# A neighbourhood-attention layer: one more unit by seven products, shorter filler in each attention cycle, and other orders of the first loads and of the output rows' splits

## The chip, the cores and the metric

The kernel runs on one core of a Trainium2 chip. The metric is the device time of one execution in microseconds, the median of several runs. In the profile PE is TensorE's matmuls, PEld its weight loads, DVE is VectorE, ACT is ScalarE, POOL is GpSimd and SP issues nearly all transfers.

## What is computed

One encoder layer on 2048 tokens (a grid of 32 rows by 64 columns) with 1024 features and 16 heads of 64. All in float32:

```python
h = rmsnorm(x, norm_0)
q, k, v, gate = split(h @ w_in_0, 4)                # 1024 x 4096
# each token attends to 8 rows x 16 columns of the grid around it
s = (q . k) / 8 + bias[head, row offset, column offset]
p = softmax(s)                                      # over the 128 keys
o = p . v
x = x + (o * silu(gate)) @ w_out_0                  # 1024 x 1024
out = rmsnorm(x, norm_f)
```

## The kernel before

Each large matrix product is done in three matmuls per tile: an operand is split into a high part (ScalarE copies it, rounded) and a low part (VectorE subtracts the high part), and high x high, low x high and high x low are summed in one PSUM bank. So each operand tile costs one operation of ScalarE and one of VectorE on 512 columns. In the code these are h and l, woh and wol (output weights), gh and gl (gated attention rows), qh and ql (queries).

There are four stages.

1. `stage_one` loads x transposed in blocks (`land`, `spot`), computes the values for the first half of the tokens and then keys, queries and gates for it. Its first rows wait for data from HBM: `load_v0` and `load_x` issue the first weights and blocks on SP in a written order, `split_v` makes high and low parts of the value weights, `values_of` runs the matmuls of one block of 128 features.
2. `stage_two` does the same for the second half of the tokens. Both compute a unit (a kind k, q or g and 256 output features for 1024 tokens) with `seven_products`: seven products of quarter blocks, 84 matmuls, where the plain way takes 96. Stage two does so for the units in `units_two`; those left over (`halves`) become filler for stage three.
3. The attention stage is a loop of 33 cycles, numbered here as m in the code. Cycle m transposes the probabilities of the strip before (`turns(m-1)`, 44 small matmuls into six banks `ph`, copied to `pta` by three operations each of ScalarE and VectorE), computes the scores of the next (`scores(2m)` and `scores(2m+1)`, eight banks `s`), and then multiplies the strip before by its values (`values`, bank `o`). A strip is a pair of heads and a group of eight grid rows. Cycles 0 to 7 take the first row group of all eight head pairs, 8 to 23 the two middle ones, 24 to 31 the last. Even cycles from 8 to 22 also build tables of bias and mask (`em`) on GpSimd.
   VectorE adds the bias to the scores and takes the maximum, ScalarE takes the exponential and its sum, VectorE the reciprocal (L1040), and `normalise` scales the eight tiles of a cycle by it on GpSimd (L1044), four after the first pair of scores and four after the second.
   Between `values` of one cycle and `turns` of the next TensorE runs filler, so that it need not wait for that chain: matmuls of `projections()` (the halves) and, once these are used up, of `outputs()`. `feed(n)` runs n of them; the table `amount` says how many in each cycle, `dense` in the first 25. A group of filler is 24 matmuls into one bank (`pp` or `po`); at its end `give` or `add_rows` empties the bank. `consume(1)` splits one prefetched tile of weights.
4. `outputs()` multiplies the rows by the output weights: 32 turns of 24 matmuls. Before a row tile's first turn `split_og` makes gh and gl of it, two operations of 512 columns on each engine. `add_rows` adds x (`y`, VectorE) and squares (`xr`, ScalarE). `run_roots` computes an inverse root in eight tiny operations of VectorE, and two more scale the rows.

The order on each engine is the order in which the code is written: nothing is rescheduled. `clock` counts filler matmuls; `store(key, lag, f)` puts off a step until the clock has gone on by `lag`. A tile of weights may be split when the clock has gone on by 32 since its load was issued.

Of the kernel before, what the change touches and what calls it, by code (L numbers as in the profile page):

```python
# [70 lines left out]
def build(ctx, tc, x, xr, xt, wg, rpb, last, w_out, n0, nf, masks, out):  # L71
# [58 lines left out]
    onesr = one.tile([128, 128], F32R, name="onesr")  # L130
    rt = one.tile([128, 16], F32, name="rt")
    g0 = one.tile([128, NK], F32, name="g0")
    accs = [one.tile([128, 512], F32, name=f"acc{i}") for i in range(2)]
# [24 lines left out]
    def load_item(it):  # L158
        kind, a, b = it
        t = raws[it] = raw([128, 512], F32, "raw")  # L160
        asked_at[it] = clock[0]
# [44 lines left out]
    def stats(c):  # L206
        ss = rows.pop(c)
        m = tiny.tile([128, 8], F32, name="m")[:, :4]
        nc.vector.tensor_tensor(m, ss[:, 0:8:2], ss[:, 1:8:2], OP.add)
        nc.vector.tensor_scalar(m, m, 1.0 / D, EPS, op0=OP.mult, op1=OP.add)  # L210
        rsqrt(rt[:, 4 * c:4 * c + 4], m, 4)

    dgs = {}
# [48 lines left out]
    AHEAD = 5  # L262
    clock = [0.0]
    freed = set()
    state = dict(used=0, loaded=0, half=-1, done_halves=0, event=0.0)
# [264 lines left out]

    def split_v(u, a, b, ks=(0, 1)):
        t = VR[u, a, b].rearrange("p (k c) -> p k c", c=256)
        if a == 0 and ks[0] == 0:
# [3 lines left out]
        nc.scalar.activation(h, t[:, k], AF.Copy)  # L537
# [28 lines left out]
    def stage_one():  # L566
# [219 lines left out]
    def stage_two():  # L786
# [9 lines left out]
        def also(n, i):  # L796
            if n == 0:
                if i == 0:
                    load_ahead()
                    load_e(0, xp)[0]()  # L800
                elif i == 1:
                    load_e(0, xp)[1]()
                    load_masks()
# [166 lines left out]

    def load_e(p, pool_=None):
# [65 lines left out]

    def normalise(i):
        st = ST.pop(i)
        nc.vector.reciprocal(st[:, 8:12], st[:, 4:8])  # L1040
        for j, C in enumerate(pairs[i][2]):
            for s in range(2):
                o = 8 + 2 * j + s
                nc.gpsimd.tensor_scalar(X[i, C][s], X[i, C][s], st[:, o:o + 1], 0.5, op0=OP.mult, op1=OP.mult)  # L1044

# [234 lines left out]
    ready = dict(loaded=2, split=1, res=RES_EARLY)  # L1280

    def outputs():
        loaded_at = {1: -1e9}

# [4 lines left out]
        def ahead(k, i=0):  # L1289
            n = ready["loaded"]  # L1290
            if n < tiles and place[n] <= k + 4 and og_ready(n):
                load_og(n)
                loaded_at[n] = clock[0]
# [84 lines left out]
    def begin(m):  # L1378
# [11 lines left out]
        if m == 0:  # L1390
            bias(0, 0, 2)
            later_loads(load_e(order[1][0]), 5, 3)

# [17 lines left out]
    for m in range(cycles + 1):  # L1411
        a = amount[m]
        begin(m)
        feed(a * 0.35)
        if m:
            normalise(2 * m - 1)
        middle(m)
        if m:
            quiet[0] = True
            for k in range(3):  # L1420
                consume(1 + (m == 1), turn=True)
                feed(a * 0.11)
                if k == 1:
# [3 lines left out]
            if quiet[0]:  # L1427
                consume(1, turn=True)
                feed(a * 0.12)
                quiet[0] = False  # L1430
            else:
                feed(a * 0.12)
        else:
            feed(a * 0.45)
        feed(a * 0.2, 8)
        if m:
# [11 lines left out]
        if m:  # L1448
            values(2 * m - 2)
            values(2 * m - 1)  # L1450
        n = next_sums(m)
        if 0 < m and n and order[m][1] < 2:
            for f in load_e(order[n][0]):
                f()
# [52 lines left out]
```

## Time and profile before

| | |
|---|---|
| median of 3 runs | 1062.33 us (1062.28 to 1062.53) |
| profiled execution | 1062.42 us, span 1060.6 us |
| PE busy | 1048.6 us (99%) |
| VectorE busy | 725.7 us (68%) |
| ScalarE busy | 518.5 us (49%) |
| GpSimd busy | 312.9 us (30%) |
| granted TensorE clock | 0.999 |

The profile is that of one execution; its rows give the start from the span's begin and the duration, both in microseconds, then engine, line and operation, `out<-in` by the program's names, and in brackets how long the engine idled before and what released it. Matmul records overlap, so a matmul's cost is read from the distance of starts. In the attention stage the letter F below stands for the start of a cycle's first filler matmul.

### The profile page before, as it was taken

How to read it: one execution, taken by the hardware profiler on the slowest of the kernel's cores; microseconds unless marked ns; L12 is line 12 of the kernel's file. 1: busy time of each engine (PE TensorE's matmuls, PEld its weight loads, DVE VectorE, ACT ScalarE, POOL GpSimd, SP SyncE). 2: the span in 40 equal slices, each digit the busy share in tenths (PEclk: the TensorE clock that was granted, in tenths of full speed). 3: DMA queues.
4: the chain of work that ended last, by engine and by line, in shares of the span. 5: the costliest groups of instructions: out<-in, count | busy, mean ns of one | idle time of the engine just before them, and what ended most of it. 6: DMA issues, size and time to landing. Idle time of an engine off the chain costs nothing.

```text
span 1060.6 us, 20997 instructions
## 1 busy us (share of the span) xinstructions
PE 1048.6 (99%) x7608; PEld 877.1 (83%) x7608; DVE 725.7 (68%) x1593; ACT 518.5 (49%) x1218; POOL 312.9 (30%) x392
## 2 busy tenths in 40 slices
PE   8999999999999999999999999999999999999997
PEld 6888888887888888888888888888887888888886
DVE  5476888768897625666576667766778777686654
ACT  7645344333343334333265656666767656445422
POOL 0000221322311000000157775665756642213200
PEclk9999999999999999999999999999999999999999
DMA  8733655353635433533798778886987788777352
GB/s 309 227 100 108 190 202 179 126 149 119 184 120 154 120 100 89 170 99 129 234 300 262 239 238 246 269 268 207 297 280 251 222 282 273 255 243 247 105 155 80
DMA packets 129184, 207.58 MB, mean 196 GB/s; under 512 B 11768, under 2 KB 55544, under 8 KB 129080
## 3 DMA queue, kind: packets, MB, share of 16 engines
q1 hardware_dynamic: 128648, 205.84, 62.5%
q8 instruction: 60, 0.98, 0.4%
q10 hardware_dynamic: 432, 0.40, 0.1%
q14 instruction: 44, 0.36, 0.1%
HBM read 147.47 MB, written 58.72 MB: 194 GB/s over the span
## 4 chain that ended last, share of the span: by engine, by line
PE 91%; DVE 4%; issue 1%; POOL 1%; DMA 1%; ACT 0%; SPq 0%; POOLq 0%; DVEq 0%
PE pp L434 30%; PE pv L555 16%; PE s L1021 7%; PE o L1123 7%; PE po L1324 5%; PE po L1326 5%; PE po L1322 5%; PE pp L382 4%; PE pp L378 4%; PE pp L380 4%; PE ph L1101 4%; DVE f L417 1%; POOL x L1044 1%; DMA land<-in_xt_dram 1%; POOL em L987 1%
## 5 line engine op out<-in xcount | busy, mean ns | idle before, releaser
L1044 POOL TENSOR_SCALAR x<-x,st 128x360 f32<-128x360 f32 (+5 forms) x256 | 176.1, 706 | 222.9 <-DVE st L1040 205.0
L434 PE MATMUL pp<-h,f 128*128 128x512 f32 x576 | 186.6, 390 | 0.0
L1035 ACT ACTIVATE x<-x,st 128x360 f32<-128x360 f32 (+5 forms) x256 | 151.3, 593 | 23.7 <-DVE st L1029 23.7
L454 POOL TENSOR_TENSOR tmp<-tmp,rb 128x512 f32<-128x512 f32 x36 | 58.6, 1628 | 270.1 <-DVE tmp L452 209.4
L987 POOL TENSOR_TENSOR em<-e,mk 128x264 f32<-128x264 f32 (+3 forms) x94 | 78.0, 864 | 192.1 <-DMA mk<-in_masks_dram 189.4
L434 PEld LDWEIGHTS pp<-h,f 128*128 128x128 f32 x576 | 108.2, 188 | 22.2
L1029 DVE CUSTOM_DVE_ANT_0 x<-s,em 128x360 f32<-128x360 f32 (+5 forms) x256 | 123.8, 538 | 0.6 <-POOL em L987 0.6
L434 PE MATMUL pp<-t,f 128*128 128x512 f32 x480 | 121.7, 390 | 0.3
L434 PE MATMUL pp<-l,f 128*128 128x512 f32 x288 | 112.2, 389 | 0.0
L434 PEld LDWEIGHTS pp<-t,f 128*128 128x128 f32 x480 | 90.0, 188 | 19.6 <-DVE u L447 1.1
L1324 PE MATMUL po<-woh,gl 128*128 128x512 f32 x252 | 99.2, 394 | 1.5 <-DVE gl L1188 1.5
L1326 PE MATMUL po<-wol,gh 128*128 128x512 f32 x252 | 98.9, 393 | 0.0
L1322 PE MATMUL po<-woh,gh 128*128 128x512 f32 x252 | 98.9, 393 | 0.0
L1077 DVE COPY pta<-ph 120x512 f32<-120x512 f32 (+5 forms) x96 | 57.8, 641 | 55.4 <-PE ph L1101 55.4
L555 PE MATMUL pv<-wh,h 128*128 128x512 f32 x256 | 88.4, 391 | 1.9 <-ACT h L519 1.4
L555 PE MATMUL pv<-wh,l 128*128 128x512 f32 x256 | 88.2, 390 | 0.0
L555 PE MATMUL pv<-wl,h 128*128 128x512 f32 x256 | 88.2, 390 | 0.0
L1077 ACT ACTIVATE pta<-ph 120x512 f32<-120x512 f32 (+5 forms) x96 | 49.7, 558 | 77.0 <-PE ph L1101 76.8
L1123 PEld LDWEIGHTS o<-pta,vt 120*64 120x64 f32 (+2 forms) x1792 | 80.9, 138 | 7.4 <-DVE st L1029 5.4
L1123 PE MATMUL o<-pta,vt 120*64 120x128 f32 (+5 forms) x1792 | 85.3, 253 | 0.0
L417 DVE TENSOR_TENSOR f<-raw,f 128x512 fp32r<-128x512 f32 x90 | 69.7, 775 | 22.4 <-ACT f L416 22.4
L1021 PE MATMUL s<-kt,qh 64*128 64x480 f32 (+5 forms) x512 | 83.0, 372 | 0.5 <-DVE pta L1077 0.5
(157 smaller groups left out, 1959.5 us busy)
## 6 DMA issues: line engine op xcount, KB each, us to landing
raw<-in_wg_dram SPq DMA_DIRECT2D x126, 256.0 KB, 5.0
row<-in_xr_dram SPq DMA_DIRECT2D x32, 256.0 KB, 4.0
vd<-v SPq DMA_DIRECT2D x32, 256.0 KB, 2.4
k_hi<-hi SPq DMA_DIRECT2D x32, 256.0 KB, 2.5
k_lo<-lo SPq DMA_DIRECT2D x32, 256.0 KB, 2.9
sgd<-sg SPq DMA_DIRECT2D x32, 256.0 KB, 4.1
qr<-qd SPq DMA_DIRECT2D x32, 256.0 KB, 5.0
sgt<-sgd SPq DMA_DIRECT2D x32, 256.0 KB, 5.1
```

The costliest lines, as they stand in the source:

```text
L434: nc.tensor.matmul(B[n, P], t[:, int(m == 2), c], x[k][int(m == 1)], start=P in (1, 6, 5) and k == 0 and m == 0, stop=k == 3 and m == 2, s ...
L555: nc.tensor.matmul(ps[t], a[:, o], b, start=k == 0 and m == 0, stop=k == NK - 1 and m == 2)
L987: (nc.gpsimd if attending[0] or not s else nc.vector).tensor_tensor(sh(t), E[p, s][:, u0 + 4:u1 + 4, v0 + 8:v1 + 8].rearrange("p u (s v) - ...
L1021: nc.tensor.matmul(pst[s], qq[a, qs], kk[a, :r1 - r0, c0:c1].rearrange("p r (s c) -> p s r c", c=8), start=(m == 0), stop=(m == 2))
L1029: nc.vector.tensor_tensor_reduce(X[i, C][s], pst[s], EM[p, ROW_TYPE[T], COL_TYPE[C], s], -1.0, 1e38, OP.add, OP.min, st[:, o:o + 1])
L1035: nc.scalar.activation(X[i, C][s], X[i, C][s], AF.Exp, bias=st[:, o:o + 1], scale=-1.0, accum_out=st[:, 4 + o:5 + o])
L1044: nc.gpsimd.tensor_scalar(X[i, C][s], X[i, C][s], st[:, o:o + 1], 0.5, op0=OP.mult, op1=OP.mult)
L1077: (nc.vector.tensor_copy if h else lambda o, i_: nc.scalar.activation(o, i_, AF.Copy))(t[:k, h, b * 512:b * 512 + w], banks_[b, h][:k, :w])
L1123: nc.tensor.matmul(to.rearrange("d (h q) -> d h q", q=64) if nq > 64 else to, vt[:k, strip, s * 64:s * 64 + 64], t[:k, h, at:at + 64] if n ...
L1322: nc.tensor.matmul(p, gh, woh[q, j], start=(i == 0), stop=False)
L1324: nc.tensor.matmul(p, gl, woh[q, j], start=False, stop=False)
L1326: nc.tensor.matmul(p, gh, wol[q, j], start=False, stop=(i == NK - 1))
```

## The change

The parts of it:

- `units_two` has a seventh unit, ("k", 2), which leaves `halves`: 96 filler matmuls become 84 in stage two.
- `dense` is 24.2 where it was 28, with 1.5 more in even and 1.5 less in odd cycles from 8 to 23. In each cycle `feed` runs 10 before the second `normalise` and shares the rest out anew.
- The factor one half of the gate moves from `normalise` into the values (`rth`). The second `normalise` of a cycle does two of its four tiles on ScalarE.
- Ages of loads count 26 per cycle beside the filler (`now`), against 36 instead of 32.
- Rows of the output are split by `split_rows` in the place of a `consume`, no longer by `ahead` during the attention.
- At the start VectorE makes the first high part of one value weight, and the second block of value weights comes in halves, with one block of x ahead of the second halves.
- `load_e` loads 11 of 15 rows of the bias for the first row group.

```diff
-    units_two = [(k, j) for j in range(2) for k in "kqg"]
-    halves = [(k, j, 1, c) for j in range(2, 4) for g in (("k", "q", "g") if j == 2 else ("k", "qg")) for c in (2, 3) for k in g]
+    units_two = [(k, j) for j in range(2) for k in "kqg"] + [("k", 2)]
+    halves = [(k, j, 1, c) for j in range(2, 4) for g in (("q", "g") if j == 2 else ("k", "qg")) for c in (2, 3) for k in g]
...
+    def now():
+        return clock[0] + 26 * runs[0]
...
-            if attending[0] and clock[0] - asked_at[items[state["used"]]] < 32 and not asked:
+            if attending[0] and now() - asked_at[items[state["used"]]] < 36 and not asked:
...
-        nc.scalar.activation(v, p, AF.Copy, scale=rt[:, t:t + 1] if t < 8 else 1.0)
+        nc.scalar.activation(v, p, AF.Copy, scale=rth[:, t:t + 1] if t < 8 else 0.5)
...
         for b in (1, 2, 3):
-            for a in range(2):
-                load_v0(0, a, b, ev([128, 512], F32, "raw") if b == 3 else None)
-            for k in (2 * b, 2 * b + 1):
-                load("x%d1" % (k // 4 + 1), k % 4)
+            for j in range(2):
+                for a in range(2):
+                    if b == 1:
+                        load_v0(0, a, b, cols=parts_[j])
+                    elif j == 0:
+                        load_v0(0, a, b, ev([128, 512], F32, "raw") if b == 3 else None)
+                load("x%d1" % (b // 2 + 1), (2 * b + j) % 4)
...
+                    if h == 0:
+                        split_v(0, 1, 0, (0,), nc.vector)
                     split_to(*(t[:, parts_[h]] for t in X1["B11"][0]), land["x11"][0][:, parts_[h]], gain("x11", 0))
                     if h == 0:
-                        split_v(0, 0, 0, (0,))
-                        split_v(0, 1, 0, (0,))
+                        split_v(0, 0, 0, (0,), fresh=False)
...
-            nc.sync.dma_start(t, rpb[2 * p + s])
+            nc.sync.dma_start(t[:, r0 * 32:r1 * 32], rpb[2 * p + s][:, r0 * 32:r1 * 32])
...
-    def normalise(i):
+    def normalise(i, both=False):
...
-                nc.gpsimd.tensor_scalar(X[i, C][s], X[i, C][s], st[:, o:o + 1], 0.5, op0=OP.mult, op1=OP.mult)
+                if both and j:
+                    nc.scalar.activation(X[i, C][s], X[i, C][s], AF.Copy, scale=st[:, o:o + 1])
+                else:
+                    nc.gpsimd.tensor_scalar(X[i, C][s], X[i, C][s], st[:, o:o + 1], 1.0, op0=OP.mult, op1=OP.mult)
...
+    def split_rows():
+        n = ready["split"]
+        if n < ready["loaded"] and "turn" in ready and place[n] <= ready["turn"] + 3 and now() - late["loaded_at"][n] >= 40 and whole(n) \
+                and sum(1 if hasattr(g, "rearrange") else 2 for g in G.values()) <= 6:
+            split_og(n)
...
-            near = 2 if quiet[0] else -1
-            if n < ready["loaded"] and place[n] <= k + near and clock[0] - loaded_at[n] >= 28 and whole(n):
+            ready["turn"] = k
+            if ended[0] and n < ready["loaded"] and place[n] <= k + 2 and now() - loaded_at[n] >= 28 and whole(n):
...
-    dense, end_of_it = 28.0, 24
+    dense, end_of_it = 24.2, 24
...
+    for m in range(8, 24):
+        amount[m] += 1.5 if m % 2 == 0 else -1.5
...
-        a = amount[m]
+        a = amount[m] - 10
         begin(m)
-        feed(a * 0.35)
+        feed(10)
         if m:
-            normalise(2 * m - 1)
+            normalise(2 * m - 1, True)
         middle(m)
         if m:
             quiet[0] = True
             for k in range(3):
-                consume(1 + (m == 1), turn=True)
-                feed(a * 0.11)
+                if not split_rows():
+                    consume(1 + (m == 1), turn=True)
+                feed(a * 0.17)
```

In the order of instructions the filler between `values` of one cycle and `turns` of the next was 28 matmuls in most cycles up to 22 (24 or 32 in some), with the end of a group four matmuls earlier in each cycle than in the one before. Now it is 24 in every cycle from 5 to 24, even and odd: 16 that end a group and 8 that begin the next. From cycle 25 on the counts are as before (48 to 59), but for one matmul.

ScalarE, in the cycle in which the second output tile begins (20 before, 19 now), from the last two exponentials to the first copy; qh is made of the queries, gh of gated rows, woh of output weights, xr is the square of y. Before:

```order
L1035 ACTIVATE x_9005,st<-x_9005,st 128x360
L1035 ACTIVATE x_9006,st<-x_9006,st 128x360
L519 ACTIVATE qh<-qr 128x512
L194 ACTIVATE woh<-raw 128x512
L1187 ACTIVATE gh<-ograw 128x512 x2
L194 ACTIVATE woh<-raw 128x512 x2
L1223 ACTIVATE xr,st_9099<-y 128x512
L1077 ACTIVATE pta<-ph_9135 120x512
```

Now:

```order
L1052 ACTIVATE x_8849,st<-x_8849,st 128x360
L1052 ACTIVATE x_8850,st<-x_8850,st 128x360
L1062 ACTIVATE x_8849<-x_8849,st 128x360
L1062 ACTIVATE x_8850<-x_8850,st 128x360
L527 ACTIVATE qh<-qr 128x512
L1207 ACTIVATE gh<-ograw 128x512 x4
L195 ACTIVATE woh<-raw 128x512 x2
L1243 ACTIVATE xr,st_8947<-y 128x512
L1097 ACTIVATE pta<-ph_8967 120x512
```

Two scalings stand ahead of qh, and the splits of two row tiles (four gh) stand in one cycle, where one stood in each of two.

VectorE in cycle 23, from the reciprocal to the first copy; st are the eight operations of a root, y with po empties a bank, y with acc scales finished rows. Before:

```order
L1220 TENSOR_TENSOR y<-po,xr 128x512
L1040 RECIPROCAL st<-st 128x4
L520 SCALAR_TENSOR_TENSOR ql<-qr,qh 128x512
L1188 TENSOR_TENSOR gl<-ograw,gh 128x512 x2
L1237 TENSOR_SCALAR st_9099<-st_9099 128x1
...
L1244 SCALAR_TENSOR_TENSOR st_9099<-st_9099 128x1
L1252 SCALAR_TENSOR_TENSOR y<-y,st_9099,acc_172 128x512
L1252 SCALAR_TENSOR_TENSOR y<-y,st_9099,acc_173 128x512
L1077 COPY pta<-ph_9822 120x512
```

Now:

```order
L1057 RECIPROCAL st<-st 128x4
L528 SCALAR_TENSOR_TENSOR ql<-qr,qh 128x512
L1208 TENSOR_TENSOR gl<-ograw,gh 128x512 x2
L1257 TENSOR_SCALAR st_8947<-st_8947 128x1
...
L1264 SCALAR_TENSOR_TENSOR st_8947<-st_8947 128x1
L1240 TENSOR_TENSOR y<-po,xr 128x512
L1272 SCALAR_TENSOR_TENSOR y<-y,st_8947,acc_173 128x512
L1272 SCALAR_TENSOR_TENSOR y<-y,st_8947,acc_174 128x512
L1097 COPY pta<-ph_9853 120x512
```

The bank is emptied behind the root, no longer ahead of the reciprocal; in cycles 19 to 24 it now always stands behind the reciprocal.

SP at the start, from the third block of x (land is a block of x, raw a tile of value weights). Before:

```order
L509 DMA land<-in_xt_dram 128x512
L529 DMA raw<-in_wg_dram 128x512 x2
L509 DMA land<-in_xt_dram 128x512 x2
L529 DMA raw<-in_wg_dram 128x512 x2
L509 DMA spot<-in_xt_dram 128x512 x2
```

Now:

```order
L517 DMA land<-in_xt_dram 128x512
L537 DMA raw<-in_wg_dram 128x256 x2
L517 DMA land<-in_xt_dram 128x512
L537 DMA raw<-in_wg_dram 128x256 x2
L517 DMA land<-in_xt_dram 128x512
L537 DMA raw<-in_wg_dram 128x512 x2
```

Four loads of half size stand where two stood, with a block of x between them.

More of the change, by code (lines that the diff above doesn't have):

```diff
@@ L131, in build @@
     rt = one.tile([128, 16], F32, name="rt")
+    rth = one.tile([128, 8], F32, name="rth")
     g0 = one.tile([128, NK], F32, name="g0")
@@ L160, in load_item @@
         t = raws[it] = raw([128, 512], F32, "raw")
-        asked_at[it] = clock[0]
+        asked_at[it] = now()
         if kind == "x":
@@ L211, in stats @@
         rsqrt(rt[:, 4 * c:4 * c + 4], m, 4)
+        if c < 2:
+            nc.vector.tensor_scalar(rth[:, 4 * c:4 * c + 4], rt[:, 4 * c:4 * c + 4], 0.5, None, op0=OP.mult)
     dgs = {}
@@ L263, in build @@
     clock = [0.0]
+    runs = [0]
+    def now():
+        return clock[0] + 26 * runs[0]
     freed = set()
@@ L529, in load_v0, with split_v @@
         by.dma_start(VR[key][:, cols], wg[KINDS["v"] + 2 * u + a, :, o + cols.start:o + cols.stop])
-    def split_v(u, a, b, ks=(0, 1)):
+    def split_v(u, a, b, ks=(0, 1), by=None, fresh=True):
         t = VR[u, a, b].rearrange("p (k c) -> p k c", c=256)
-        if a == 0 and ks[0] == 0:
+        if ks[0] == 0 and (a == 0 if by is None else a == 1) and fresh:
             W[u, b] = wp([128, 2, 512], F32R, "wh"), wp([128, 2, 512], F32R, "wl")
@@ L536, in split_v @@
         h, l = W[u, b][0][:, k, s], W[u, b][1][:, k, s]
-        nc.scalar.activation(h, t[:, k], AF.Copy)
+        if by is None:
+            nc.scalar.activation(h, t[:, k], AF.Copy)
+        else:
+            by.tensor_copy(h, t[:, k])
         nc.vector.tensor_tensor(l, t[:, k], h.bitcast(F32), OP.subtract)
@@ L799, in also @@
                     load_ahead()
[L800 removed]
+                    load_e(0, 0, xp)[0]()
                 elif i == 1:
[L802 removed]
+                    load_e(0, 0, xp)[1]()
                     load_masks()
@@ L969, in load_sg, with load_e @@
         nc.sync.dma_start(SG[p, T], sgd[p][:, T * 512:T * 512 + 512])
-    def load_e(p, pool_=None):
+    def load_e(p, ty, pool_=None):
+        r0, r1 = (4, 15) if ty == 0 else (0, 15)
         def rows(s):
@@ L1043, in normalise @@
                 o = 8 + 2 * j + s
-                nc.gpsimd.tensor_scalar(X[i, C][s], X[i, C][s], st[:, o:o + 1], 0.5, op0=OP.mult, op1=OP.mult)
+                if both and j:
+                    nc.scalar.activation(X[i, C][s], X[i, C][s], AF.Copy, scale=st[:, o:o + 1])
+                else:
+                    nc.gpsimd.tensor_scalar(X[i, C][s], X[i, C][s], st[:, o:o + 1], 1.0, op0=OP.mult, op1=OP.mult)
     def split(C):
@@ L1280, in build @@
     ready = dict(loaded=2, split=1, res=RES_EARLY)
+    def split_rows():
[3 more added lines that the diff above has]
+            split_og(n)
+            ready["split"] += 1
+            return True
     def outputs():
-        loaded_at = {1: -1e9}
+        loaded_at = late["loaded_at"] = {0: -1e9, 1: -1e9}
         def more_rows():
@@ L1292, in ahead @@
                 load_og(n)
-                loaded_at[n] = clock[0]
+                loaded_at[n] = now()
                 ready["loaded"] += 1
@@ L1391, in begin @@
             bias(0, 0, 2)
-            later_loads(load_e(order[1][0]), 5, 3)
+            later_loads(load_e(order[1][0], 0), 5, 3)
     def middle(m):
@@ L1427, in build @@
             if quiet[0]:
-                consume(1, turn=True)
-                feed(a * 0.12)
+                if not split_rows():
+                    consume(1, turn=True)
+                feed(a * 0.19)
                 quiet[0] = False
             else:
-                feed(a * 0.12)
+                feed(a * 0.19)
         else:
-            feed(a * 0.45)
-        feed(a * 0.2, 8)
+            feed(a * 0.7)
+        feed(a * 0.3, 8)
         if m:
@@ L1450, in build @@
             values(2 * m - 1)
+        runs[0] += 1
         n = next_sums(m)
         if 0 < m and n and order[m][1] < 2:
-            for f in load_e(order[n][0]):
+            for f in load_e(order[n][0], ROW_TYPE[order[n][1]]):
                 f()
```

## The prediction

> **What bounds the kernel now.** I read the page first, then who TensorE waited for, then the rows in order of time where it waits.
>
> ```profile
> span 1060.6 us, 20997 instructions
> PE 1048.6 (99%) x7608; PEld 877.1 (83%) x7608; DVE 725.7 (68%) x1593; ACT 518.5 (49%) x1218; POOL 312.9 (30%) x392
> ...
> PE po L1324 <- DVE gl L1188: 1.5, 2, 1.1
> PE pv L555 <- ACT h L519: 1.4, 1, 1.4
> ```
>
> TensorE is busy 99% of the span, and the two largest waits named are 1.5 and 1.4 us. So the kernel is a queue of matmuls, and a change can win only by taking matmuls out or by closing the few gaps; it can lose by opening new ones. The profiled execution took 1062.42 us (1.8 us lie around its span), 0.1 us over the median of the runs shown, 1062.33. A measurement of this kernel tells about 0.2%, 2.1 us, from no change.
>
> The price of a matmul is the distance of starts, since a record overlaps the next:
>
> ```profile
> 154.75 2.88 PE L434 MATMUL pp<-t,f 128*128 128x512 f32 x12
> 157.47 0.39 PE L434 MATMUL pp<-h,f 128*128 128x512 f32 x1
> ```
>
> Twelve matmuls take 157.47 - 154.75 = 2.72 us, 0.227 each.
>
> One cycle of the attention stage (cycle 15) shows what the filler covers:
>
> ```profile
> 724.86 0.50 PE L378 MATMUL pp<-h,w 128*128 128x512 f32 x1
> 725.58 0.58 ACT L1035 ACTIVATE x<-x,st 128x360 f32<-128x360 f32 x1
> 726.16 0.61 ACT L519 ACTIVATE qh<-qr 128x512 fp32r<-128x512 f32 x1
> 726.29 0.18 DVE L1040 RECIPROCAL st<-st 128x4 f32<-128x4 f32 x1 [0.62 <-ACT x L1035]
> 726.81 1.03 DVE L520 SCALAR_TENSOR_TENSOR ql<-qr,qh 128x512 fp32r<-128x512 f32 x1 [0.34 <-ACT qh L519]
> 731.44 1.50 PE L1101 MATMUL ph<-ident,x 64*120 64x64 f32 x44
> 732.19 1.83 DVE L1077 COPY pta<-ph 120x512 f32<-120x512 f32 x3 [2.95 <-PE ph L1101]
> 732.21 1.58 ACT L1077 ACTIVATE pta<-ph 120x512 f32<-120x512 f32 x3 [3.70 <-PE ph L1101]
> 732.75 0.73 PE L1021 MATMUL s<-kt,qh 64*128 64x360 f32 x4
> 733.37 0.83 PE L1021 MATMUL s<-kt,qh 64*128 64x480 f32 x4
> ```
>
> I count times from F, the first filler matmul (724.86). The last exponential ends at F+1.3, the reciprocal at F+1.6, qh starts at F+1.3 and ql at F+1.95. The 28 fillers end at F+6.6, when the transposes start; the copies pta follow 0.77 later on both engines, and the scores 1.31 later. VectorE had been idle 2.95 us and ScalarE 3.70 us before the copies: that is the room for more work or less filler. The scores write into the banks that the copies free, so a late copy stops TensorE almost at once.
>
> **The change, part by part.**
>
> *Seven products for one more unit.* 96 filler matmuls go, 84 come in stage two: 12 fewer, **-2.7 us**. The unit runs as the six before it do; their largest group has no idle time before it, so I add nothing:
>
> ```profile
> L434 PE MATMUL pp<-h,f 128*128 128x512 f32 x576 | 186.6, 390 | 0.0
> ```
>
> *The gaps that go.* In cycles 20 and 21 the second matmul of a new output tile waits for its low half gl:
>
> ```profile
> 796.30 0.39 PE L1322 MATMUL po<-woh,gh 128*128 128x512 f32 x1
> 797.09 0.51 PE L1324 MATMUL po<-woh,gl 128*128 128x512 f32 x1 [0.40 <-DVE gl L1188]
> 809.69 0.50 PE L1322 MATMUL po<-woh,gh 128*128 128x512 f32 x1
> 811.30 0.50 PE L1324 MATMUL po<-woh,gl 128*128 128x512 f32 x1 [1.10 <-DVE gl L1188]
> ```
>
> 0.79 and 1.61 instead of 0.23: 0.56 + 1.38 = 1.9 us. Three more gaps lie in cycles 23, 16 and 29:
>
> ```profile
> 843.13 0.73 PE L1021 MATMUL s<-kt,qh 64*128 64x360 f32 x4
> 844.42 0.75 PE L1021 MATMUL s<-kt,qh 64*128 64x480 f32 x4 [0.38 <-DVE pta L1077]
> 744.90 1.84 PE L1101 MATMUL ph<-ident,x 64*120 64x64 f32 x42
> 746.55 0.43 PE L1021 MATMUL s<-kt,qh 64*128 64x360 f32 x1
> 950.92 0.38 PE L1021 MATMUL s<-kt,qh 64*128 64x288 f32 x1
> 951.47 0.41 PE L1021 MATMUL s<-kt,qh 64*128 64x288 f32 x2 [0.17 <-DVE pta L1077]
> ```
>
> The first costs 0.7 (in cycle 15 the scores of 360 and of 480 start 0.62 apart, here 844.42 - 843.13 = 1.29), the second 0.3 (1.65 from transposes to scores, not 1.31), the third 0.5. All of the old gaps together: **-3.4 us**. I take them out whole and put the new ones in.
>
> *The new gaps.* Now each cycle from 5 to 24 holds 24 fillers, 16 that end a group and 8 that begin the next; the order shows this for even and odd cycles alike, so the 1.5 that the table adds and takes changes nothing. The transposes start 4 x 0.227 = 0.9 us earlier, at F+5.7, the copies are due at F+6.45, the scores at F+7.0, their second pair at F+7.6. At the same time ScalarE gets two of the scalings, ahead of qh: they wait for the reciprocal (F+1.6), with qh, the high halves and the copies queued behind them, and take about 0.4 each (estimate: a 512-column copy pta takes 1.58/3 = 0.53, these have 360 columns). So qh ends at F+3.0 and ql starts at F+3.05, 1.1 us later than now; everything behind ql on VectorE moves with it. In all, 2 us of the 2.95 are gone in a plain cycle. That still fits: cycles without splits cost nothing, and the transposes no longer wait for GpSimd, whose eight scalings become six. If the cover of a plain cycle should go, each 0.1 us costs 20 x 0.1.
>
> It does not fit where the list is long. Prices:
>
> ```profile
> 824.61 0.66 DVE L520 SCALAR_TENSOR_TENSOR ql<-qr,qh 128x512 fp32r<-128x512 f32 x1
> 825.19 0.68 DVE L195 TENSOR_TENSOR wol<-raw,woh 128x512 fp32r<-128x512 f32 x1
> 797.56 1.57 DVE L195 TENSOR_TENSOR wol<-raw,woh 128x512 fp32r<-128x512 f32 x2
> 799.05 0.68 DVE L1220 TENSOR_TENSOR y<-po,xr 128x512 f32<-128x512 f32 x1
> 799.76 0.63 ACT L1223 ACTIVATE xr<-y 128x512 f32<-128x512 f32 x1 [2.77 <-DVE y L1220]
> 840.65 0.20 DVE L1237 TENSOR_SCALAR st<-st 128x1 f32<-128x1 f32 x1
> 842.36 1.41 DVE L1252 SCALAR_TENSOR_TENSOR y<-y,st,acc 128x512 f32<-128x512 f32 x2
> 843.69 1.75 DVE L1077 COPY pta<-ph 120x512 f32<-120x512 f32 x3
> ```
>
> An operation of VectorE on 512 columns costs 0.6 to 0.75 from start to start; I take 0.63 in odd cycles, where GpSimd ends six scalings by F+3.3 (below), and 0.7 in even ones, where it builds tables. The eight small ones of a root take 842.36 - 840.65 = 1.7, the two scalings behind them 1.3. Note xr: ScalarE squares y (0.7 with its read-out), and stands in order before its own copies. So y, then xr, then the first copy (0.6) is a chain.
>
> - Cycle 19: ql at 3.05, four gl, two wol, y: 8 x 0.63, y ends at F+8.1. The new tile's gl is late by 0.3 at its matmul. xr ends at 8.8, the copy at 9.4, against scores due at 7.6 + 0.3: 1.5. Together 1.8.
> - Cycle 20: ql, three wol, y, from 3.05 with GpSimd running (ql 1.0): y ends at 6.8, copy at 8.1 against 7.05: 1.0.
> - Cycle 21: the same at 0.63: copy at 7.45, 0.4.
> - Cycle 23: ql, two gl, root 1.7, y, two scalings 1.3: copies from F+8.6, the first ends at 9.25 against 7.6: 1.6.
> - Cycle 24: the same without gl: 0.4 (narrower scores).
>
> Sum 5.2 us. Bounds: 2 if an operation is 0.55 and ql starts early; 10 with the dear prices of the second rival. I take **+5.2**, from the nearest rows. The last eight cycles have 48 and more fillers (one has 24 and little else), and the root pair that cost 0.5 falls into a cycle with five fillers more: nothing.
>
> *The start.* The third block of rows is awaited now:
>
> ```profile
> 9.93 0.63 ACT L537 ACTIVATE wh<-raw 128x512 fp32r<-128x512 f32 x1 [1.43 <-DMA raw<-in_wg_dram]
> 11.41 1.41 ACT L519 ACTIVATE h<-land,g 128x512 fp32r<-128x512 f32 x2 [0.85 <-DMA land<-in_xt_dram]
> 12.18 1.20 PE L555 MATMUL pv<-wh,h 128*128 128x512 f32 x4 [1.38 <-ACT h L519]
> ```
>
> The last arrival is the row block (11.41), and one operation follows it. After the change the weights come in halves and the row block before the second halves, but wh still takes a whole tile: the same bytes are needed, the last to arrive is a weight, and wh (0.63) then h follow it. If the last byte comes at the same time that costs 0.6; if smaller pieces come 0.8 sooner it gains 0.2; if two more issues on SP delay them, 1.2. I take **+0.5**. What VectorE takes over at the first block lies before this wait and is hidden by it (1.4 us of cover).
>
> The rest has one answer. The factor one half moved into v, two tiny operations (rth) and shorter loads of the bias rows touch nothing that TensorE waits for; ages counted with 26 per cycle let weights be split in another cycle, which is in the lists above. The DMA queues carry the same in cycles 0.9 us shorter; no wait of TensorE names a transfer.
>
> Sum: 1062.4 - 2.7 - 3.4 + 5.2 + 0.5 = **1062.0 us**.
>
> [...]
>
> ```profile
> 724.12 5.33 POOL L1044 TENSOR_SCALAR x<-x,st 128x360 f32<-128x360 f32 x8 [2.68 <-DVE st L1040]
> ```
>
> **The rivals.**
>
> *The queues keep up (faster, 0.28).* If ScalarE's two scalings delay ql by 0.5, not 1.1, and VectorE runs at 0.58, the five cycles cost 0.9 + 0.2 + 0 + 0.9 + 0 = 2.0, and the start 0: 1062.4 - 2.7 - 3.4 + 2.0 = 1058.3. For it: ScalarE idled 3.7 us in cycle 15. Against it: ql waits for qh already now. It decides where ql starts before F+2.6.
>
> *VectorE is held by GpSimd (slower, 0.15).* If GpSimd still works while the long lists run, each operation with two operands in SBUF (ql, gl, wol) is held as ql was, 0.37: seven of them in cycle 19, three more in 20 (its ql is counted so), four in 21, three in 23, one in 24, 18 x 0.37 = 6.7 together: 1068.7. [...] For it: ql's 1.03. Against it: GpSimd has two scalings fewer. It decides where GpSimd is busy past F+4 in odd cycles.
>
> *The change does other than it says (0.05).* Were stage two's seventh unit starved (its weights come while the masks and first keys load), it would give back its 2.7 us and more, 1065 or over; were only the start to gain its 1.4 us of waiting, 1060. I split this 0.03 slower, 0.02 faster.
>
> **How the numbers follow.** Forecast, within 0.2%: 0.52; its own range is 1059.9 to 1064.2. Faster 0.28 + 0.02 = 0.30, slower 0.15 + 0.03 = 0.18. The range 1058.2 to 1064.9 takes in the first rival's price and the way to the second up to 40%, and leaves out about 2 in 10.
>
> **What would show it.** Right: 12 matmuls of 512 columns fewer; F to transposes 5.7 in cycles 9 to 24; ql near F+3; gaps before the scores of cycles 19, 20 and 23 of 1 to 2 us, named by pta on ScalarE or VectorE; the third block at 12.5 to 12.9. Wrong: ql before F+2.6, or gaps of under 2 us in all, or waits for transfers in the attention stage.

## The result, and the profile after

The changed kernel takes 1069.7 us (median of 5 runs, 1069.2 to 1070.9) against 1062.3 for the kernel before: 1.0074 of its time, 95% interval 1.006 to 1.0089. It is slower by 7.4 us; forecast were 1062.0 and a range from 1058.2 to 1064.9. In the two profiled executions the span went from 1060.6 to 1068.2 us, and the 7.6 us between them are followed here. Times are medians of all executions and ratios are of the fast ones: of the four of before_two_on_scalare, below, one took 2297 us and is not in its ratio.

The head of the page of the changed kernel (span, then busy time and number of instructions of each engine), and its answer on what TensorE waited for (total, times, longest):

```profile
span 1068.2 us, 20961 instructions
PE 1052.0 (98%) x7596; PEld 876.8 (82%) x7596; DVE 739.8 (69%) x1608; ACT 551.3 (52%) x1285; POOL 261.9 (25%) x328
...
PE s L1038 <- issue: 2.3, 2, 2.0
PE s L1038 <- ACT pta L1097: 2.0, 3, 0.8
PE s L1038 <- DVE pta L1097: 2.0, 2, 1.6
...
PE s L1038 <- DVE lo L373: 0.7, 1, 0.7
```

Twelve matmuls are gone (7608 to 7596), and still TensorE is busy 3.4 us longer, and it waits for the copies pta before its scores. With the 2.7 us of the missing matmuls that is 6.1 us more than its work accounts for; 3.4 of them are a slower clock, which the windows show further down, and the rest this head does not tell. GpSimd has 51 us less to do, ScalarE 33 more.

The loss lies in the attention cycles. From the first scores to the filler of the last cycle the changed kernel needs 10.7 us more than the kernel before, once 93 fillers fewer at 0.227 are taken off. Ahead of that it has 81 matmuls more and comes 0.3 us earlier than these account for, and behind it only 0.1 us differs: -2.7 - 0.3 + 10.7 = 7.7. Cycle by cycle, the time that a cycle takes beyond that of an undisturbed one (the spaces between the starts of its parts, against those of its neighbours) is 0.5, 0.8, 0.3, 0.9, 3.2 and 4.5 us in cycles 1, 2, 6, 10, 16 and 20, together 10.2, and 1.9, 1.6 and 1.1 in cycles 19, 23 and 24, together 4.6. The first six have one thing in common: GpSimd makes mask products (`em`) in them while VectorE splits weights. Cycles 4, 8, 12, 14, 18 and 22 make products too, without a weight split beside them, and lose nothing.

Cycle 16 before, in order of time: VectorE's ql and three weight splits, then GpSimd's scalings and mask products:

```profile
741.78 0.66 DVE L520 SCALAR_TENSOR_TENSOR ql<-qr,qh 128x512 fp32r<-128x512 f32 x1
742.36 2.28 DVE L195 TENSOR_TENSOR wol<-raw,woh 128x512 fp32r<-128x512 f32 x3
742.06 4.11 POOL L1044 TENSOR_SCALAR x<-x,st 128x480 f32<-128x480 f32 x4 [2.17 <-DVE st L1040]
746.14 5.48 POOL L987 TENSOR_TENSOR em<-e,mk 128x360 f32<-128x360 f32 x6
```

The same cycle after (F is 746.75), with the copies and the scores that wait for them:

```profile
749.99 1.21 DVE L528 SCALAR_TENSOR_TENSOR ql<-qr,qh 128x512 fp32r<-128x512 f32 x1 [1.67 <-ACT qh L527]
751.13 4.38 DVE L196 TENSOR_TENSOR wol<-raw,woh 128x512 fp32r<-128x512 f32 x3
755.43 1.74 DVE L1097 COPY pta<-ph 120x512 f32<-120x512 f32 x3
745.97 3.84 POOL L1064 TENSOR_SCALAR x<-x,st 128x360 f32<-128x360 f32 x6 [8.67 <-DVE st L1057]
749.77 7.29 POOL L1004 TENSOR_TENSOR em<-e,mk 128x360 f32<-128x360 f32 x6
756.16 0.77 PE L1038 MATMUL s<-kt,qh 64*128 64x480 f32 x4 [1.56 <-DVE pta L1097]
```

Before, the products started at 746.14, when VectorE was done with its splits. With two scalings gone to ScalarE, GpSimd starts them at F+3.0, and ql, held up behind those same two scalings on ScalarE, starts at F+3.24. The two meet: three splits take 4.38 us instead of 2.28, six products 7.29 instead of 5.48. The copies start at F+8.7, two microseconds late.

Cycle 20 has y behind the splits as well, and ScalarE's copies behind y:

```profile
804.82 7.28 POOL L1004 TENSOR_TENSOR em<-e,mk 128x360 f32<-128x360 f32 x6
806.18 4.37 DVE L196 TENSOR_TENSOR wol<-raw,woh 128x512 fp32r<-128x512 f32 x3
810.48 0.68 DVE L1240 TENSOR_TENSOR y<-po,xr 128x512 f32<-128x512 f32 x1
811.26 0.42 PE L1038 MATMUL s<-kt,qh 64*128 64x360 f32 x1 [2.05 <-issue]
812.45 0.97 PE L1038 MATMUL s<-kt,qh 64*128 64x360 f32 x3 [0.77 <-ACT pta L1097]
```

The profile names no releaser for the wait of 2.05 us. The scores start 0.1 us after y was done, and in cycle 19 the profile names y for such a wait (a row of it stands further down); that y, which empties a bank, ended this one too is inferred.

Then comes a second charge. The windows around cycle 16's wait (the stretch, its length, TensorE's busy time and matmuls, then the granted clock, the DMA share and GB/s):

```profile
756.00:756.50 0.50, 0.34 (x2) 1.00 0.99 314
757.50:758.00 0.50, 0.50 (x6) 0.63 1.11 163
758.00:758.50 0.50, 0.50 (x7) 0.50 1.54 208
760.00:760.50 0.50, 0.50 (x10) 0.50 1.00 410
761.00:761.50 0.50, 0.50 (x17) 0.96 1.07 434
```

Some 1.5 us after the wait has ended, TensorE's clock is halved for about 3.4 us, so a wait of 1.56 us costs another 1.7. In cycle 20 the clock is halved for as long, from 1.0 us after the wait of 2.05 us. Of the 10.2 us, 3.4 are this.

### The profile page after: what moved, and what is told of

The parts are those of the page before. It is cut to its first block, busy times and chain, and to the rows that moved or that the text cites. A ratio compares the mean times of both kernels' runs of the same rounds, so it can differ in the third digit from the quotient of the medians.

```text
span 1068.2 us, 20961 instructions
## 1 busy us (share of the span) xinstructions
PE 1052.0 (98%) x7596; PEld 876.8 (82%) x7596; DVE 739.8 (69%) x1608; ACT 551.3 (52%) x1285; POOL 261.9 (25%) x328
## 4 chain that ended last, share of the span: by engine, by line
PE 86%; DVE 6%; DMA 2%; ACT 2%; issue 2%; POOL 1%; SPq 0%; DVEq 0%; ACTq 0%; POOLq 0%
PE pp L442 31%; PE pv L566 16%; PE s L1038 7%; PE o L1143 6%; PE po L1354 5%; PE po L1352 5%; PE po L1350 5%; PE ph L1121 3%; PE pp L390 3%; PE pp L388 3%; PE pp L386 3%; DVE x L1046 1%; DVE f L425 1%; DVE wol L196 1%; ACT x L1052 1%
## 5 line engine op out<-in xcount | busy, mean ns | idle before, releaser
L442 PE MATMUL pp<-h,f 128*128 128x512 f32 x608 | 196.7, 389 | 0.0
L1064 POOL TENSOR_SCALAR x<-x,st 128x480 f32<-128x480 f32 (+5 forms) x192 | 110.6, 593 | 261.9 <-DVE st L1057 240.4
L1004 POOL TENSOR_TENSOR em<-e,mk 128x264 f32<-128x264 f32 (+3 forms) x94 | 92.6, 1019 | 211.1 <-DMA mk<-in_masks_dram 210.3
L442 PEld LDWEIGHTS pp<-h,f 128*128 128x128 f32 x608 | 114.1, 188 | 23.7
L442 PE MATMUL pp<-t,f 128*128 128x512 f32 x506 | 128.5, 390 | 0.3
L442 PE MATMUL pp<-l,f 128*128 128x512 f32 x304 | 118.3, 389 | 0.0
L442 PEld LDWEIGHTS pp<-t,f 128*128 128x128 f32 x506 | 94.8, 188 | 20.8 <-DVE u L455 1.1
L1038 PE MATMUL s<-kt,qh 64*128 64x480 f32 (+5 forms) x512 | 86.0, 382 | 7.6 <-issue 2.3
L425 DVE TENSOR_TENSOR f<-raw,f 128x512 fp32r<-128x512 f32 x95 | 73.2, 771 | 22.4 <-ACT f L424 22.4
L1038 PEld LDWEIGHTS s<-kt,qh 64*128 64x128 f32 x512 | 62.1, 192 | 15.8 <-ACT pta L1097 3.9
```

Source lines behind the costliest of these rows:

```text
L425: nc.vector.tensor_tensor(t[:, 1], src, t[:, 0].bitcast(F32), OP.subtract)
L442: nc.tensor.matmul(B[n, P], t[:, int(m == 2), c], x[k][int(m == 1)], start=P in (1, 6, 5) and k == 0 and m == 0, stop=k == 3 and m == 2, s ...
L1004: (nc.gpsimd if attending[0] or not s else nc.vector).tensor_tensor(sh(t), E[p, s][:, u0 + 4:u1 + 4, v0 + 8:v1 + 8].rearrange("p u (s v) - ...
L1038: nc.tensor.matmul(pst[s], qq[a, qs], kk[a, :r1 - r0, c0:c1].rearrange("p r (s c) -> p s r c", c=8), start=(m == 0), stop=(m == 2))
```

## The experiments

Theory one: mask products and weight splits, both with two operands in SBUF, hold each other up (*collision*). Theory two: ScalarE's scalings make ql and the list behind it late, and VectorE's speed plays no part (*late list*). The net figures below are those of the attention cycles against the kernel before, counted as the 10.7 above.

| run | time, us | ratio to before, interval | net, us |
|---|---|---|---|
| the changed kernel | 1069.7 | 1.0074, 1.006 to 1.0089 | +10.7 |
| eight_on_gpsimd | 1060.5 | 0.9989, 0.9979 to 0.9998 | +1.6 |
| two_more_on_gpsimd | 1066.1 | 1.0038, 1.0023 to 1.0053 | +7.3 |
| scalings_behind_qh | 1059.1 | 0.9974, 0.9963 to 0.9984 | -0.2 |
| before_two_on_scalare | 1078.7 | 1.0146, 1.0126 to 1.0167 | +16.5 |
| masks_one_operand | 1061.3 | 0.9996, 0.9986 to 1.0006 | +1.9 |
| old_row_order | 1060.8 | 0.9989, 0.9979 to 0.9998 | +1.7 |
| more_filler_late | 1062.0 | 0.9999, 0.999 to 1.0008 | +2.5 |
| filler_27 | 1078.0 | 1.015, 1.0135 to 1.0166 | +20.1 |
| seven_units_only | 1061.1 | 0.9992, 0.9983 to 1.0001 | +1.7 |
| scalare_without_masks | 1058.0 | 0.9962, 0.9948 to 0.9975 | -1.1 |
| four_more_in_23 | 1057.9 | 0.996, 0.9948 to 0.9973 | -1.7 |
| more_in_19_and_23 | 1056.6 | 0.995, 0.9937 to 0.9962 | -2.4 |

**eight_on_gpsimd.**

```
-            normalise(2 * m - 1, True)
+            normalise(2 * m - 1)
```

> The changed kernel with all eight scalings back on GpSimd (ScalarE gets none ahead of qh); seven units, 24 fillers a cycle, the start and the row order stay. Theory one (mask products collide): GpSimd is done with the scalings 1.3 us later, so its mask products start near F+4 and the weight splits of even cycles run ahead of them; ql is back at F+2. About 10 of the 14.1 us of new gaps go, and some of those in cycles 19 to 24: 1057 to 1060. Theory two (ScalarE's scalings only make ql and the list behind it late): the same edit takes the lateness away, 1057 to 1060 too. Were it neither, but the four fillers fewer in each cycle that uncover the list, the time stays at 1066 or over.

1060.5 us, 9.2 less than the changed kernel; no mask cycle is disturbed any more, and cycles 19, 23 and 24 keep nearly 6 us (3.7 in cycle 19, of which a half clock makes 1.7). Its cycle 16:

```profile
747.80 2.27 DVE L196 TENSOR_TENSOR wol<-raw,woh 128x512 fp32r<-128x512 f32 x3
750.93 5.49 POOL L1004 TENSOR_TENSOR em<-e,mk 128x360 f32<-128x360 f32 x6
```

The splits end before the products start. So the loss of the mask cycles is the move of the two scalings, and neither the seventh unit nor the shorter filler; which half of the move, this run cannot tell.

**two_more_on_gpsimd.** Behind ScalarE's scaling of each tile, GpSimd multiplies another by one:

```
                     nc.scalar.activation(X[i, C][s], X[i, C][s], AF.Copy, scale=st[:, o:o + 1])
+                    x0 = X[i, pairs[i][2][0]][s]
+                    nc.gpsimd.tensor_scalar(x0, x0, 1.0, 1.0, op0=OP.mult, op1=OP.mult)
```

> The changed kernel with ScalarE's two scalings left where they are, and two more operations on GpSimd behind its six (two tiles multiplied by one), so that its mask products start 1.3 us later while ql stays at F+3. Theory one (collision): the first product now starts near F+4.1, one of three weight splits gets through at 0.65 us; cycles 16 and 20 lose about 0.8 us of stall each and the half clock behind it (1.65 us each): 1063 to 1067. Theory two (late ql alone): nothing gets better, 1069 to 1071.

```profile
748.42 3.63 DVE L196 TENSOR_TENSOR wol<-raw,woh 128x512 fp32r<-128x512 f32 x3
748.91 6.82 POOL L1004 TENSOR_TENSOR em<-e,mk 128x360 f32<-128x360 f32 x6
752.70 0.77 PE L1038 MATMUL s<-kt,qh 64*128 64x480 f32 x4 [0.89 <-DVE pta L1099]
```

1066.1: more work on GpSimd makes the program 3.6 us faster, as the collision has it, and as the late list cannot. One split gets through ahead of the products, at 1.07 us beside the last scaling; the wait of cycle 16 falls to 0.89 us, and no half clock follows it. The mask cycles gain 5.7 us in all. Cycles 19 and 23 lose 2.7 and 3.4, more than in the changed kernel: there GpSimd now works until F+5.0 and F+4.6, and a gl beside it takes 1.06 and 1.07 (0.68 otherwise). So the total lies in the range that was expected, but not by the expected sum.

**scalings_behind_qh.** `normalise` calls `middle` between GpSimd's scalings and ScalarE's, so that qh stands ahead of those:

```
-            normalise(2 * m - 1, True)
-        middle(m)
+            normalise(2 * m - 1, True, lambda: middle(m))
+        else:
+            middle(m)
```

> The changed kernel with ScalarE's two scalings behind qh instead of ahead of it: ql is back near F+2, and the mask products still start at F+3. Theory one (collision): of three weight splits in cycles 16 and 20 one or two still run beside the products at 1.4 us; the stalls shrink by about 1.1 us each, and the half clock goes where the stall falls under 1.4 us: 1062 to 1066. Theory two (late ql alone): the lists fit again as in the kernel before, 1057 to 1060.

1059.1, in the range of the late list, 2.9 us under that of the collision; of the mask cycles only cycle 20 still loses, 0.8 us. But the splits still run against the products:

```profile
748.68 3.26 DVE L196 TENSOR_TENSOR wol<-raw,woh 128x512 fp32r<-128x512 f32 x3 [0.46 <-ACT woh L195]
748.72 6.91 POOL L1004 TENSOR_TENSOR em<-e,mk 128x360 f32<-128x360 f32 x6
```

3.26 us instead of 2.27, 1.0 us lost, and in cycle 16 the cover takes it: ql started at F+2. Neither theory alone holds. A list that starts in time fits the cover even at the slowed speed. Whether one that starts late fits it at a better speed is what the next run asks; the changed kernel has the lateness and the slowness together.

**masks_one_operand.** The mask is left out of the bias sum, the price of the product is changed and its place is not:

```
-                sh(t), E[p, s][:, ...], sh(MK[0][:, m0:m0 + n]), OP.add)
+                nc.gpsimd.tensor_scalar(sh(t), e, 1.0, 0.0, op0=OP.mult, op1=OP.add)
```

> The changed kernel with ScalarE's two scalings where they are (ql late as in it, near F+3) and GpSimd's mask products made from one operand (the mask is left out of the bias sum, so the result lacks it); they start as early as in the changed kernel. Collision theory (the two-operand products double VectorE's splits): the splits run at 0.65 to 0.8 us, the stalls of cycles 1, 2, 6, 10, 16 and 20 go, 1058 to 1061. Late-list theory (speed plays no part): 1068 to 1070. Of the collision only a part: 1063 to 1066.

```profile
748.22 0.80 DVE L528 SCALAR_TENSOR_TENSOR ql<-qr,qh 128x512 fp32r<-128x512 f32 x1 [1.67 <-ACT qh L527]
748.95 2.95 DVE L196 TENSOR_TENSOR wol<-raw,woh 128x512 fp32r<-128x512 f32 x3
748.00 4.71 POOL L1006 TENSOR_SCALAR em<-e 128x360 f32<-128x360 f32 x6
```

1061.3, just above the range of the collision. ql is as late as in the changed kernel, the products start as early, and five of the six mask cycles are undisturbed; cycle 20, where y stands behind the splits, keeps 1.4 of its 4.5 us. The late list without the slow splits is thus worth nothing in the five and at most 1.4 us in cycle 20. The 10.2 us need both: 0.8 are left where the list starts in time, 1.4 where the splits are less slow. The splits are slowed here too, to 0.98 each and not to the 0.65 to 0.8 expected: an operation of one operand holds them as well, but it is the shorter one (4.71 us for six, not 7.29).

**before_two_on_scalare.** The kernel before, with `normalise` and the factor one half of the changed kernel and nothing else of it.

> The kernel before with only the move of two scalings of each second pair to ScalarE, ahead of qh (and the factor one half moved into v for that); 28 fillers, the old row order and start. Theory one (collision): mask products start 1.3 us or more earlier and meet the weight splits; with 0.9 us more cover than the changed kernel has, cycles 16 and 20 stall by about 1 us each: 1064 to 1067. Theory two (late ql alone): the 28 fillers cover 1.1 us in plain cycles, cycles 20, 21 and 23 get about 0.5 worse each: 1062.5 to 1064.

```profile
752.30 4.37 DVE L196 TENSOR_TENSOR wol<-raw,woh 128x512 fp32r<-128x512 f32 x3
750.95 7.26 POOL L990 TENSOR_TENSOR em<-e,mk 128x360 f32<-128x360 f32 x6
757.32 0.79 PE L1024 MATMUL s<-kt,qh 64*128 64x480 f32 x4 [2.65 <-DVE pta L1083]
```

1078.7, far beyond both. The move alone costs 16.5 us of attention time with 28 fillers, more than the whole change. Four fillers more do not cover it: in cycle 16 the emptying of a filler group stands ahead of the reciprocal in that kernel, and ql starts at F+5.3 (751.21 against 745.95). Most is lost in cycles 1, 16 and 20, which have products.

**old_row_order.** eight_on_gpsimd with the kernel before's rule for splitting the output rows (`near` back in `ahead`, `split_rows` never).

> Eight scalings on GpSimd, as in the run of that name (1060.5), with the kernel before's rule for when gl and gh of a new row tile are split; seven units, 24 fillers and the new start stay. If the new rule's list opened the 3.7 us of cycle 19, they go, and the old waits for gl in cycles 20 and 21 come back, 0.6 and 1.4 us as before plus up to 0.9 each for the four fillers less: 1058 to 1061, no clear difference. If the new rule is a loss: 1057 or less; if it pays: 1062 or more.

1060.8: no difference. Where the new rule loses 3.7 us in cycle 19, the old one loses 2.4 there and 1.1 in cycle 20, without a half clock. The waits for gl did not come back where they were expected: cycle 21 loses nothing.

**seven_units_only.** The kernel before, with two lines of the change:

```
-    units_two = [(k, j) for j in range(2) for k in "kqg"]
+    units_two = [(k, j) for j in range(2) for k in "kqg"] + [("k", 2)]
-    dense, end_of_it = 28.0, 24
+    dense, end_of_it = 24.2, 24
```

> The kernel before with the seventh unit moved into stage two and 24 fillers a cycle, and nothing else (eight scalings on GpSimd, old start, old row order, old feeding). By its terms: 12 matmuls less, -2.7; the start nothing; the waits for gl in cycles 20 and 21 up to 0.9 us longer each and the late copies of cycle 23 too: 1060 to 1062, no clear difference from the kernel before. If the new start or the new row order is what the 1060.5 of eight scalings on GpSimd rests on: 1062.5 or more.

1061.1, the time that was worked out, though not by its terms: the wait for gl in cycle 21 goes instead of growing, and cycle 19 opens by 2.3 us. The seventh unit brings its 2.7 us, and 24 fillers a cycle give 1.7 of it back, in cycles 19, 23 and 24 and net of the old waits that go. The start and the row order add nothing to it that these runs can tell (1060.5 with both, 1060.8 without the row order).

**more_filler_late** and **filler_27**, both on scalings_behind_qh:

```
+    for m in (19, 20, 23, 24):
+        amount[m] += 6
```

> The changed kernel with ScalarE's scalings behind qh (1059.1 in the run of that name) and six fillers more in each of cycles 19, 20, 23 and 24, taken from the last eight cycles, which hold 48 and more. If its remaining 3.4 us of gaps (cycles 19, 20, 23, 24) are only too little cover, they fall to about 1: 1056 to 1057.5. If a group's end that falls late in a cycle makes its emptying late instead: 1059 or more.

```
-    dense, end_of_it = 24.2, 24
+    dense, end_of_it = 27.0, 24
```

> The changed kernel with the scalings behind qh and 27 fillers in each cycle instead of 24, so that groups no longer end at the same place. Cover alone: the gaps of cycles 19 to 24 shrink by 0.7 each: 1056.5 to 1058. If group ends wander into the lists: 1059 to 1062.

Both miss: 1062.0 and 1078.0. In the first the gaps of cycles 20, 23 and 24 go and that of cycle 19 shrinks from 1.8 to 0.6 us, but an output row is finished earlier, and its root falls into cycle 22, where products are made, and costs 5.9 us there:

```profile
828.18 0.20 DVE L1259 TENSOR_SCALAR st<-st 128x1 f32<-128x1 f32 x1
828.80 0.22 DVE L1262 SCALAR_TENSOR_TENSOR st<-st 128x1 f32<-128x1 f32 x1
829.05 1.02 DVE L1263 SCALAR_TENSOR_TENSOR st<-st 128x1 f32<-128x1 f32 x1
830.11 1.01 DVE L1264 SCALAR_TENSOR_TENSOR st<-st 128x1 f32<-128x1 f32 x1
831.15 0.78 DVE L1265 SCALAR_TENSOR_TENSOR st<-st 128x1 f32<-128x1 f32 x1
831.97 0.78 DVE L1266 SCALAR_TENSOR_TENSOR st<-st 128x1 f32<-128x1 f32 x1
826.35 6.39 POOL L1004 TENSOR_TENSOR em<-e,mk 128x360 f32<-128x360 f32 x6
834.86 1.17 PE L1038 MATMUL s<-kt,qh 64*128 64x480 f32 x4 [4.61 <-DVE pta L1099]
```

The last four operations of a root, on one column, take 0.16 to 0.22 us in the median in the kernels before and after (one of them 0.45 at its longest) and 1.02, 1.01, 0.78 and 0.78 here; their neighbour of one tensor operand (828.18) stays at 0.20. So the price did not go with the columns: 0.6 to 0.9 us more on one column, 0.7 to 0.8 on 512. The last of the four ends at 832.75 and the last of GpSimd's six products at 832.74. The operation at 828.80 has two operands as well and was not slowed (0.22), though the products ran from 826.35 on. This is the plainest sign that the two hold each other up, and it comes from a run made for another reason; what the hold consists of was not shown. In filler_27 long lists fall into several cycles between 17 and 26: two roots in cycle 21, a root beside products in cycle 22.

**scalare_without_masks**, **four_more_in_23**, **more_in_19_and_23.** ScalarE takes two scalings, behind qh, only where no products follow; then one and two places of filler:

```
+            tb = m < cycles and (order[m][0], ROW_TYPE[order[m][1]], 0, 0) not in EM
+            normalise(2 * m - 1, not tb, lambda: middle(m))
...
+    for m, n in ((19, 5), (20, -5), (23, 6)):
+        amount[m] += n
```

(the second has only the pair of cycle 23.)

> The changed kernel with two scalings on ScalarE, behind qh, only in cycles in which GpSimd has no mask products to make; in the others all eight are on GpSimd, so that the products start after the weight splits. Collision theory: cycle 20 loses its last stall (0.85 us with the scalings behind qh in every cycle), 19, 23 and 24 keep 3.0 us: 1057.5 to 1059, or 0.2% to 0.4% under the kernel before. If the last 0.85 us of cycle 20 came from elsewhere: 1059 to 1060, the same as with the scalings behind qh.

> As scalare_without_masks, with more filler in cycle 23 only (27 instead of 24, behind the last cycle with mask products, so that no list before it moves). If the 1.2 us of cycle 23 (a root, two scalings, copies) are too little cover: 0.7 us less, 1056.8 to 1058.3. If the group that ends later in cycle 24 costs it again: no change.

> As four_more_in_23, with two fillers more in cycle 19 and none added elsewhere. Cover only: the 1.8 us of cycle 19 fall by 0.5: 1056.3 to 1058. If the emptying of the output bank, which now stands ahead of a weight split there, lets the scores start earlier too: 1 us less.

1058.0, 1057.9 and 1056.6, all within their ranges; the second's 0.7 us in cycle 23 are there in its trace, its time differs from the first's by less than the runs tell. The last is faster than both kernels, by 0.5% of the kernel before. What its TensorE still waits for, a first wait of 1.2 us ahead of the loads aside (pv belongs to the start):

```profile
PE pv L566 <- ACT h L527: 0.5, 2, 0.3
PE s L1038 <- ACT pta L1099: 0.2, 1, 0.2
```

## Why the prediction was wrong

**Right.** The 12 matmuls (-2.7 us). 24 fillers in each cycle, and 5.67 us from F to the transposes (cycle 19 apart, where a gl was late). ql at F+3.05 was forecast; it came at F+3.4, 3.05 and 3.24 in cycles 19, 20 and 16. The gaps of cycles 19 and 23, forecast as 1.8 and 1.6, were 1.9 and 1.6. The list of cycle 19, and the score that waited for y:

```profile
790.98 0.69 DVE L528 SCALAR_TENSOR_TENSOR ql<-qr,qh 128x512 fp32r<-128x512 f32 x1 [1.67 <-ACT qh L527]
791.58 2.49 DVE L1208 TENSOR_TENSOR gl<-ograw,gh 128x512 fp32r<-128x512 f32 x4
795.94 1.22 PE L1038 MATMUL s<-kt,qh 64*128 64x360 f32 x4 [0.30 <-DVE y L1240]
```

Four gl at 0.62 each is the 0.63 of the prediction. Some of the sum is luck: cycles 21 and 24, forecast as 0.4 each, were nothing and 1.1, and the old gaps, taken out as 3.4, were 4.0 (counted cycle by cycle as above).

**The step that failed** is the price of an operation in the even cycles: "0.7 in even ones, where it builds tables". It was 1.46. That one number made cycle 20 a gap of 1.0 instead of 2.8 (4.5 with the half clock behind it), and cycles 1, 2, 6, 10 and 16, where weights are split beside products too, stood in no list. All in all the mask cycles were priced at 1.0 us and took 10.2, the others at 4.2 and took 4.6.

Rows with a price of this size were in the trace of before. In stage two VectorE's f runs beside GpSimd's product of tmp and, elsewhere, alone:

```profile
112.82 1.77 DVE L417 TENSOR_TENSOR f<-s,f 128x512 fp32r<-128x512 f32 x1
118.62 0.69 DVE L417 TENSOR_TENSOR f<-raw,f 128x512 fp32r<-128x512 f32 x1
112.37 1.67 POOL L454 TENSOR_TENSOR tmp<-tmp,rb 128x512 f32<-128x512 f32 x1 [1.23 <-DMA raw<-in_wg_dram]
```

The prediction took its measure from ql beside a scaling (1.03 us in cycle 15 against 0.66 in cycle 22, 0.37 more), because that was the neighbour in the attention cycles. There the products ran mostly beside VectorE's copies pta, which read PSUM and took 0.58 to 0.69 us each in cycle 16, but not always. In cycle 8 one weight split met them and took 1.20 us, where the one ahead of it took 0.68:

```profile
633.40 0.68 DVE L190 TENSOR_TENSOR w<-raw,w 128x512 fp32r<-128x512 f32 x1
635.54 1.20 DVE L190 TENSOR_TENSOR w<-raw,w 128x512 fp32r<-128x512 f32 x1 [1.46 <-ACT w L189]
635.32 5.10 POOL L987 TENSOR_TENSOR em<-e,mk 128x360 f32<-128x360 f32 x5
```

Why the others came so late, the prediction did not ask: GpSimd was busy with eight scalings until then. It counted what ScalarE gets by the move and not what GpSimd does with the time it gains.

**The second rival** (held by GpSimd, 1068.7) came within 1 us of the time and had the right mechanism in the wrong place. Its test was GpSimd busy past F+4 in odd cycles; in cycles 19, 21 and 23, which have the long lists, the scalings end at F+3.3 or earlier (F+3.3 was the forecast, six eighths of the 5.33 us that eight take from 724.12), and gl ran at 0.62. It put 18 holds of 0.37 there. The changed kernel shows holds of 0.8, in even cycles, and by products that start early rather than scalings that end late. That its time came so near is therefore luck. Its 0.15 and a range that stopped at 40% of the way to it were too little for a slowing that stood in the rows and spoke against the change.

**The half clock** was in no term: 3.4 of the 10.2 us. No wait of the attention stage of before is longer than 1.1 us (1.10, gl in cycle 21), so its trace could not show it.

**The start** was forecast as +0.5 and measured -0.3:

```profile
11.74 0.50 PE L566 MATMUL pv<-wh,h 128*128 128x512 f32 x1 [0.48 <-ACT h L527]
```

But over seven profiles with the new start this matmul begins at 11.3 to 12.7 us, over three with the old one at 11.77, 12.05 and 12.18. The sign stays open; it is less than the arrivals scatter.

## What to carry to other kernels

Work taken from an engine is not gone: ask what that engine does earlier now, and which two-operand instructions of VectorE it will meet there (here weight splits, three of them in 4.38 us instead of 2.28). For the price of such a meeting look through the whole trace for the same pair of operations, not only near the change. And a gap on TensorE was not priced by its length alone here (1.56 us of waiting cost another 1.7); one that is longer than any in the trace before has no price there.

## What the runs showed of the hardware

Where several stood in a row, a VectorE operation with two SBUF operands beside GpSimd's two-operand products went from 0.65 to 1.46 us on 512 columns (weight splits, cycles 19 and 16 of the changed kernel), and from 0.16 to 0.22 us to 0.78 to 1.02 on one (a root, more_filler_late). In cycle 16 three splits took 2.27 us ahead of the products (eight_on_gpsimd), 2.95 beside one-operand ones (masks_one_operand) and 4.38 beside two-operand ones.

TensorE's clock was halved behind waits of 1.56 and 2.05 us (cycles 16 and 20 of the changed kernel), for 3.4 us each, from 1.5 and 1.0 us after the wait's end, which costs up to 1.7. It was at 0.50 as well at 758.0 and at 760.0 in before_two_on_scalare, whose wait of 2.65 us ended at 757.32. After waits of 1.10 us in cycle 21 and of 1.38 us at the start of the kernel before it stayed at 1.00, and so it did after 0.77 us in cycle 23 of the changed kernel. The length of one wait is not all of it: in two_more_on_gpsimd, where cycle 16 waits 0.89 us at full clock (46 matmuls of values behind the wait take 2.22 us, 26 ahead of it 1.28), the granted clock of the profiled execution was 0.995 all the same (0.999 in the kernel before), with waits of 1.04 and 0.79 us close together in cycle 20 and of 0.84 and 0.78 us in cycle 23. The half clock in cycle 19 of eight_on_gpsimd came with waits of 0.52 and 0.80 us. Which lengths and distances bring it was not shown.
